# Forgetting attention on TensorE: two heads scored in the two halves of the array's rows, values formed once per pair

## The chip, the cores and the metric

The kernel runs on one core of one Trainium2 chip. The metric is device time in microseconds of one execution; lower is better. The shape is fixed: one sequence of 512 tokens, width 1024, one launch for the whole program.

## What is computed

Two transformer-like blocks in a row. Only the attention of the second block changes. It has 16 heads of 64 channels, 512 queries and keys, a causal mask, and a "forget" term: a running sum `c` per head and key that is added to the scores before the softmax.

```
def forgetting_attention(q, k, v, c):
    ...
    def one_block(args):
        q_i, c_i, i = args
        s = jnp.einsum('bhqd,bhkd->bhqk', q_i, k, preferred_element_type=jnp.float32) * scale
        s = s + c_i[..., None] - c[:, :, None, :]
        qpos = i * Q_BLOCK + jnp.arange(Q_BLOCK)
        s = jnp.where(kpos[None, :] <= qpos[:, None], s, -jnp.inf)
        p = jax.nn.softmax(s, axis=-1)
        return jnp.einsum('bhqk,bhkd->bhqd', p.astype(v.dtype), v)
```

(`c_i` is the same for a whole row of scores, so the softmax doesn't see it; the kernel adds only the key's part.) Keys and queries come from projections with a norm per head; the result is multiplied by a sigmoid gate and projected by `b_w_out`.

## The kernel before, in words

**Matmuls of the projections.** All weights are fp32. A weight tile is split into a rounded part `wh` (ScalarE, L181) and the rest `wl` (VectorE, L182), an activation tile likewise into `xh` and `xl`, and each product is three matmuls of 128x128 by 128x512 (L202, L203, L204 in `mm3`). One output tile `mm` is 8 such triples. There are three pairs of `wh`/`wl` buffers, so a split waits until TensorE has finished with the pair three tiles earlier.

**Attention before.** Heads lie in pairs, 64 channels each in one tile of 128 partitions (`KN[i]`, `pairs[i]`). For each head, `stack` builds stacked operands of 128 rows: `qa` and `ka` hold the rounded part in one half of the rows and, in the other half, the rest of the query and a copy of the rounded key; `qb` and `kb` hold the rounded query against the rest of the key, and in rows 64 to 111 the forget sums against a selecting column. So `scores` of a head and a block `tb` of 128 queries is two matmuls of up to 128 rows (L1279, L1280) over the `w = 128 (tb + 1)` keys seen so far, and a bf16 matmul of a mask with the identity over the diagonal block (L1281). VectorE takes the row maximum `nmx` (L1283), `powers` is an exponential on ScalarE, `shares` multiplies by the reciprocal of the sum (GpSimd for `tb` 0 and 1, VectorE for 2 and 3, L114), `turn` transposes each 128x128 piece on TensorE (`pt`, L1305) and copies it out on ScalarE (`et`, L1307), and `values` multiplies with the values (`ao`, L1317): fp32 matmuls of 128 rows by 64 columns of the array, head A into output partitions 0 to 63, head B into 64 to 127. Each fp32 matmul of that kind stands in the trace as two records.

**What sets the order.** `weave` interleaves two generators: `main` (query and gate projections, in the order `ORDER`, after `QL` queries that run ahead) and `side` (the attention, 64 steps of one head and one block, `LAG` steps between scores and transposes, `VLAG` steps between transposes and values). `ATT` holds their weights. A scheduler then places each engine's instructions in a fixed order; at run time every engine works through its own list and waits where an operand or a buffer is not ready. PSUM has 8 banks for all of it. The last stretch, `residual("bo", ...)`, uses the gated pairs after they are split (`OS`).

One place in the first block matters for the prediction. L742 in `Core.mid` issues fp32 matmuls of 128 rows by 32 columns of the array in turn for two column groups (output partitions 0 to 31 and 32 to 63), each over 64 moving columns.

Of the kernel before, what the change touches and what calls it, by code (L numbers as in the profile page):

```python
# [8 lines left out]
F32 = mybir.dt.float32  # L9
F32R = mybir.dt.float32r  # L10
BF16 = mybir.dt.bfloat16
# [9 lines left out]
NT = 4  # L21
# [7 lines left out]
N_T = 51  # L29
N_S = 10  # L30
N_T2 = 6
XA = 14

LOOK = 2

# [22 lines left out]
def tile_two_blocks(ctx: ExitStack, tc: tile.TileContext, a: dict, out: bass.AP):  # L58
# [23 lines left out]
    def PS(name="p", shape=(128, 512)):  # L82
        return pp.tile(list(shape), F32, tag="p", name=nm(name))
# [997 lines left out]
    def bcast_a():  # L1081
# [11 lines left out]
    cmask = T("cmask", (128, 128))  # L1093
    pool.memset(cmask, 0.0)
    pool.affine_select(out=cmask, in_=cmask, compare_op=ALU.is_ge, fill=NEG, base=0,
                       pattern=[[-1, 128]], channel_multiplier=1)
    cm16 = cp.tile([128, 128], BF16, name="cm16")
    pool.tensor_copy(cm16, cmask)
    id16 = cp.tile([128, 128], BF16, name="id16")
    pool.tensor_copy(id16, ident)  # L1100


    cr = xp[-1].tile([48, 512], F32R, tag="x", name="cr")
    pool.memset(cr.bitcast(F32), 0.0)
    sel = T("sel", (48, 16))
    pool.memset(sel, 0.0)
    for q in (0, 32):
        dve.tensor_copy(sel[q:q + 16, :], ident[q:q + 16, q:q + 16])
    selr = cp.tile([48, 16], F32R, name="selr")
    dve.tensor_copy(selr, sel)  # L1110

    def forget(p):
        z = T("fz", (16, 512))
        tt(dve, z, p[:16, :], nrm["rb"][:16, :])
        ts(dve, z, z, bft[:, 0:1], ALU.add)
        e = T("fe", (16, 512))
        stt(e, z, -1.0, z, ALU.mult, ALU.min)
        f(e, e, AF.Exp)
        f(e, e, AF.Ln, bias=1.0)
        stt(e, z, 0.0, e, ALU.min, ALU.subtract)  # L1120
        on = T("on", (16, 512))
# [4 lines left out]
        stt(cr[32:48, :], cs, -1.0, cr[0:16, :].bitcast(F32), ALU.mult, ALU.subtract)  # L1126

    kqs = cp.tile([128, 2], F32, name="kqs")
    ts(dve, kqs[:, 0:1], V("kn"), -0.5, ALU.mult)
# [105 lines left out]
            i, hn = summed.pop(0)  # L1235
            pairs[i] = hn.out()

    kbs = [xp[-1].tile([128, 512], F32R, tag="kb", bufs=2, name=nm("kb")) for _ in range(2)]
    for t in kbs:
        dve.tensor_copy(t[64:112, :], cr.bitcast(F32))  # L1240
    stacks, parts = {}, []

    def stack(h):

        i, hA = divmod(h, 2)
        qn, kn = pairs[i], KN[i]
        if hA:
            pairs.pop(i)
        u = slice(64 * hA, 64 * hA + 64)
        w = slice(64 - 64 * hA, 128 - 64 * hA)  # L1250
        qa, ka, qb = (xp[-1].tile([128, 512], F32R, tag="x", name=nm(s)) for s in ("qa", "ka", "qb"))
        kb = kbs[h % len(kbs)]
        stacks[h] = (qa, ka, qb, kb)
# [20 lines left out]
    def scores(h, tb):  # L1274
        qa, ka, qb, kb = stacks[h]
        w = (tb + 1) * 128
        p = PS("sc")
        tsl = slice(tb * 128, (tb + 1) * 128)
# [3 lines left out]
        nmx = SM("nmx", 1)  # L1282
        dve.tensor_reduce(out=nmx, in_=p[:, :w], axis=AX.X, op=ALU.max, negate=True)  # L1283
        return p, nmx

    def powers(h, tb, p, nmx):
        w = (tb + 1) * 128
        e = XT("pe")
        ssum = SM("sum", 1)
        f(e[:, :w], p[:, :w], AF.Exp, bias=nmx, accum=ssum)  # L1290
        sums.append((h, tb, e, ssum))

    def shares():
        h, tb, e, ssum = sums.pop(0)
        w = (tb + 1) * 128
        rs = SM("rs", 1)
        dve.reciprocal(rs, ssum)  # L1297
        ts(pool if tb in SHARE_POOL else dve, e[:, :w], e[:, :w], rs, ALU.mult)
        es[h, tb] = e

    def turn(h, tb):
        e = es.pop((h, tb))
# [4 lines left out]
        act.copy(et[:, :(tb + 1) * 128], pt[:, :(tb + 1) * 128])  # L1307
        ets[h, tb] = et

    def values(h, tb):  # L1310
        i, hA = divmod(h, 2)
        if i not in outs:
            outs[i] = PS("ao")
        o = outs[i]
        et = ets.pop((h, tb))
        for j in range(tb + 1):
            pe.matmul(o[64 * hA:64 * hA + 64, tb * 128:(tb + 1) * 128],  # L1317
                      lhsT=v[j][h // 8][:, (h % 8) * 64:(h % 8) * 64 + 64],
                      rhs=et[:, j * 128:(j + 1) * 128], start=(j == 0), stop=(j == tb))

    def side():
        def wait(i):
            while i not in pairs:
                yield None

        yield from wait(0)
        for part in stack(0):
            part()
        for _ in range(HEADSTART):
            yield None  # L1330
        for n in range(64 + LAG + VLAG):
            m = n - LAG
            k = m - VLAG
            if n % 4 == 0 and n < 60:
                yield from wait((n // 4 + 1) // 2)
                parts.extend(stack(n // 4 + 1))
            if n < 64:
                p, nmx = scores(*divmod(n, NT))
                yield 55 + 107 * (n % NT + 1)
            if sums:  # L1340
                shares()
            if 0 <= m < 64:
                turn(*divmod(m, NT))
                yield 107 * (m % NT + 1)
            if n < 64:
                powers(*divmod(n, NT), p, nmx)
            if parts:
                parts.pop(0)()
            elif turns["g"] == 8 and len(OS) < len(OG):
                OS.append(split(OG[len(OS)]))  # L1350
            if k >= 0:
                values(*divmod(k, NT))
                if k % 4 == 3:
                    stacks.pop(k // 4)
                if k % 8 == 7:
                    i = k // 8
                    while i not in gates:
                        yield None
                    t = T("og")
                    tt(dve, t, outs.pop(i), gates.pop(i))  # L1360
                    OG.append(t)
                    if i == 7:
                        for q in range(len(OS), 8):
                            OS.append(split(OG[q]))
                yield 214 * (k % NT + 1)

    def main():
        for k in ORDER:
# [37 lines left out]
```

## Time and profile before

| what | value |
|---|---|
| median of 3 runs | 2132.24 us (2131.89 to 2133.09) |
| profiled execution, its time | 2132.8 us |
| profiled execution, its span | 2131.1 us |
| TensorE busy | 2087.4 us, 98% of the span, 11200 matmuls |
| VectorE / ScalarE / GpSimd busy | 57% / 41% / 23% |
| attention with the woven projections | about 1541 to 1727 us from the span's start |

The span runs from the first to the last instruction. A busy TensorE is not one at its peak: matmuls are pipelined, records overlap, and what a matmul costs is read from the distance between the starts of neighbours, not from its duration.

### The profile page before, as it was taken

To read this page: it belongs to the slowest core of one execution; us is meant where nothing else is said; L and a number is where in the kernel's file an instruction comes from. 1 tells how busy PE (TensorE), PEld (TensorE's weight loads), DVE (VectorE), ACT (ScalarE), POOL (GpSimd) and SP (SyncE) were. 2 spreads that over 40 slices of the span, in tenths; PEclk is the share of its full clock that TensorE was granted. 3 is DMA by queue.
4 is the path that set the end of the run, shared out by engine and by line. 5 is a ranking of instruction groups with operands and counts; after the bars stand their busy time and mean duration, and the time that the engine had idled before them with its cause. 6 is when DMAs were issued, how large, how long until landed. Compare 5 with 4: busy or idle time off the path is not lost.

```text
span 2131.1 us, 27353 instructions
## 1 busy us (share of the span) xinstructions
PE 2087.4 (98%) x11200; PEld 1710.1 (80%) x11200; DVE 1221.2 (57%) x1636; ACT 880.2 (41%) x1362; POOL 493.9 (23%) x440
## 2 busy tenths in 40 slices
PE   8998888999999999999999999999999999999999
PEld 7877677888888888888888888878877778888887
DVE  4698787555344443664654453568587765545453
ACT  5456555543323323422333232345466644323232
POOL 3555654012222222400210010120034311001000
PEclk9999989999999999999999999999999999999999
DMA  6221111332233332323232233233311112323221
GB/s 219 90 70 41 61 60 60 99 115 86 97 99 99 99 97 82 99 79 119 80 114 91 93 99 99 80 101 99 98 41 41 40 60 79 107 91 108 90 89 50
DMA packets 179190, 187.54 MB, mean 88 GB/s; under 512 B 4379, under 2 KB 169976, under 8 KB 179064
## 3 DMA queue, kind: packets, MB, share of 16 engines
q1 hardware_dynamic: 179048, 185.79, 27.1%
q8 instruction: 88, 1.44, 0.3%
q14 instruction: 38, 0.31, 0.0%
q10 hardware_dynamic: 16, 0.00, 0.0%
HBM read 183.68 MB, written 2.10 MB: 87 GB/s over the span
## 4 chain that ended last, share of the span: by engine, by line
PE 91%; DVE 5%; ACT 2%; POOL 1%; issue 1%; DMA 0%; SPq 0%; POOLq 0%; ACTq 0%; DVEq 0%
PE mm L202 26%; PE mm L203 26%; PE mm L204 26%; PE ao L1317 2%; PE mn L244 1%; PE mn L243 1%; PE mn L242 1%; DVE dec L107 1%; DVE wl L182 1%; POOL dec L107 1%; PE pt L1305 1%; DVE sc L107 1%; PE sc L1279 1%; PE ml L229 1%; PE ml L228 1%
## 5 line engine op out<-in xcount | busy, mean ns | idle before, releaser
L202 PE MATMUL mm<-xh,wh 128*128 128x512 f32 x2552 | 1000.7, 393 | 0.0
L203 PE MATMUL mm<-xl,wh 128*128 128x512 f32 x2552 | 996.1, 391 | 2.9 <-DVE xl L107 2.9
L204 PE MATMUL mm<-xh,wl 128*128 128x512 f32 x2552 | 995.9, 391 | 0.0
L181 ACT CAST wh<-raw 128x1024 fp32r<-128x1024 f32 (+2 forms) x355 | 363.7, 1025 | 782.2 <-PE mm L203 695.2
L182 DVE TENSOR_TENSOR wl<-raw,wh 128x1024 fp32r<-128x1024 f32 (+2 forms) x355 | 469.5, 1323 | 187.0 <-ACT wh L181 182.6
L203 PEld LDWEIGHTS mm<-xl,wh 128*128 128x128 f32 x2552 | 479.3, 188 | 103.1 <-DVE xl L107 3.2
L202 PEld LDWEIGHTS mm<-xh,wh 128*128 128x128 f32 x2552 | 479.1, 188 | 102.2 <-issue 1.7
L204 PEld LDWEIGHTS mm<-xh,wl 128*128 128x128 f32 x2552 | 479.3, 188 | 100.7 <-issue 0.5
L107 POOL TENSOR_TENSOR ua<-ua,rb 128x512 f32<-128x512 f32 x44 | 57.3, 1302 | 592.6 <-ACT ua L120 592.6
L107 DVE TENSOR_TENSOR x<-mm,x 128x512 f32<-128x512 f32 x64 | 44.1, 691 | 153.0 <-PE mm L204 153.0
L107 POOL TENSOR_TENSOR dec<-sc 128x256 f32<-128x256 f32 x96 | 85.6, 921 | 30.0 <-DVE sc L652 23.4
L107 POOL TENSOR_TENSOR acc<-acc,sq 128x512 f32<-128x512 f32 x42 | 66.4, 1583 | 105.1 <-ACT sq L120 84.0
L107 DVE TENSOR_TENSOR a<-mm,rb 128x512 f32<-128x512 f32 x44 | 30.4, 691 | 103.8 <-PE mm L204 103.8
L107 POOL TENSOR_TENSOR rl<-rl 128x512 f32<-128x512 f32 x32 | 49.2, 1537 | 129.1 <-ACT rl L120 129.1
L107 DVE TENSOR_TENSOR sg<-mm,ua 128x512 f32<-128x512 f32 x44 | 30.4, 690 | 83.9 <-POOL ua L107 81.4
L114 POOL TENSOR_SCALAR pe<-pe,rs 128x128 f32<-128x128 f32 (+1 forms) x32 | 31.0, 969 | 188.8 <-DVE rs L1297 183.4
L110 DVE SCALAR_TENSOR_TENSOR ua<-a,convs,ua 128x511 f32<-128x511 f32 x88 | 65.8, 748 | 4.8 <-ACT ua L120 3.3
L120 ACT ACTIVATE ua<-ua 128x512 f32<-128x512 f32 x44 | 27.8, 632 | 86.9 <-DVE ua L110 86.9
L242 PE MATMUL mn<-wh,xh 128*128 128x512 f32 x160 | 63.2, 402 | 0.0
L243 PE MATMUL mn<-wl,xh 128*128 128x512 f32 x160 | 62.9, 393 | 0.0
L244 PE MATMUL mn<-wh,xl 128*128 128x512 f32 x160 | 60.8, 390 | 0.0
L107 DVE TENSOR_TENSOR rs<-mm,rb 128x512 f32<-128x512 f32 x32 | 22.0, 688 | 60.1 <-PE mm L204 60.1
(259 smaller groups left out, 1984.0 us busy)
## 6 DMA issues: line engine op xcount, KB each, us to landing
raw<-in_ffn_w_up_dram SPq DMA_DIRECT2D x44, 1024.0 KB
raw<-in_w_ff_dram SPq DMA_DIRECT2D x32, 1024.0 KB
raw<-in_w_in_dram SPq DMA_DIRECT2D x26, 1024.0 KB
raw<-in_ffn_w_down_dram SPq DMA_DIRECT2D x18, 1024.0 KB
raw<-in_a_w_in_dram SPq DMA_DIRECT2D x12, 1024.0 KB
raw<-in_w_kvf_dram SPq DMA_DIRECT2D x8, 1024.0 KB
raw<-in_b_w_qg_dram SPq DMA_DIRECT2D x8, 1024.0 KB
raw<-in_w_up_b_dram SPq DMA_DIRECT2D x4, 1024.0 KB
```

The costliest lines, as they stand in the source:

```text
L107: e.tensor_tensor(out=o, in0=i0, in1=i1, op=op)
L110: dve.scalar_tensor_tensor(out=o, in0=i0, scalar=s, in1=i1, op0=op0, op1=op1)
L114: e.tensor_scalar(out=o, in0=i, scalar1=s1, scalar2=None, op0=op0)
L181: act.copy(hi, src)
L182: ins = dve.tensor_tensor(out=lo, in0=src, in1=hi.bitcast(F32), op=ALU.subtract)
L202: pe.matmul(ps, lhsT=lh, rhs=rh, start=start, stop=False)
L203: pe.matmul(ps, lhsT=lh, rhs=rl, start=False, stop=False)
L204: pe.matmul(ps, lhsT=ll, rhs=rh, start=False, stop=stop_)
L242: pe.matmul(pss[j], lhsT=xh[:, t0], rhs=wh[:, kk, :], start=(k + kk == 0), stop=False)
L243: pe.matmul(pss[j], lhsT=xh[:, t0], rhs=wl[:, kk, :], start=False, stop=False)
L244: pe.matmul(pss[j], lhsT=xl[:, t0], rhs=wh[:, kk, :], start=False, stop=(k + kk == nk - 1))
L1317: pe.matmul(o[64 * hA:64 * hA + 64, tb * 128:(tb + 1) * 128], lhsT=v[j][h // 8][:, (h % 8) * 64:(h % 8) * 64 + 64], rhs=et[:, j * 128:(j + ...
```

## The change

`stack` is built once per pair: the key tile and the query tile of the pair (128 partitions, both heads) are each split once into `kh`, `kl`, `qh`, `ql`. `scores` handles both heads of a pair for one block: three products of 64 rows for each head (`qh kh`, `ql kh`, `qh kl`), head A in rows 0 to 63 of the array and head B in rows 64 to 127, each into its own PSUM bank; a matmul over 48 rows that adds the forget sums; and the mask as two bf16 matmuls of 64 rows by 64 columns for each head. `values` runs once per pair, after its four blocks, and takes the two heads in turn. The steps are 32 instead of 64, `LAG` and `VLAG` are counted in those, and four queries run ahead of the weave instead of three.

```diff
-XA = 14
+XA = 18
...
-LAG = 4
-VLAG = 3
-QL = 3
-ORDER = "gqgqgqgqgqggg"
+LAG = 2
+VLAG = 1
+QL = 4
+ORDER = "gqgqgqgqgggg"
...
-ATT = (70, 72)
+ATT = (70, 66)
...
-    def stack(h):
-
-        i, hA = divmod(h, 2)
-        qn, kn = pairs[i], KN[i]
...
-        def high():
-            act.copy(ka[u, :], kn[u, :])
-            act.copy(qa[u, :], qn[u, :])
-
-        def low_k():
-            tt(dve, kb[0:64, :], kn[u, :], ka[u, :].bitcast(F32), ALU.subtract)
-            pool.tensor_copy(qb[64:112, :], selr[:, h:h + 1].bitcast(F32).to_broadcast([48, 512]))
-
-        def low_q():
-            tt(dve, qa[w, :], qn[u, :], qa[u, :].bitcast(F32), ALU.subtract)
-
-        def twice():
-            dve.tensor_copy(ka[w, :], ka[u, :].bitcast(F32))
-            dve.tensor_copy(qb[0:64, :], qa[u, :].bitcast(F32))
-
-        return [high, low_k, low_q, twice]
+    def stack(i):
+
+        qn, kn = pairs.pop(i), KN[i]
+        qh, kh, ql, kl = (RX(s) for s in ("qh", "kh", "ql", "kl"))
+        stacks[i] = (qh, ql, kh, kl)
+
+        def part(src, hi, lo):
+            act.copy(hi, src)
+            tt(dve, lo, src, hi.bitcast(F32), ALU.subtract)
+
+        return [lambda: part(kn, kh, kl), lambda: part(qn, qh, ql)]
...
-        pe.matmul(p[:, :w], lhsT=qa[:, tsl], rhs=ka[:, :w], start=True, stop=False)
-        pe.matmul(p[:, :w], lhsT=qb[:112, tsl], rhs=kb[:112, :w], start=False, stop=False)
-        pe.matmul(p[:, tsl], lhsT=id16, rhs=cm16, start=False, stop=True)
+        for n, (q, k) in enumerate(((qh, kh), (ql, kh), (qh, kl))):
+            for u in range(2):
+                pe.matmul(ps[u][:, :w], lhsT=q[half[u], tsl], rhs=k[half[u], :w], start=(n == 0), stop=False)
+        for u in range(2):
+            r = slice(64 * u, 64 * u + 48)
+            pe.matmul(ps[u][:, :w], lhsT=selr[r, 2 * i + u:2 * i + u + 1].to_broadcast([48, 128]), rhs=cr[r, :w],
+                      start=False, stop=False)
+        for n in range(2):
+            for u in range(2):
+                c0 = tb * 128 + 64 * n
+                pe.matmul(ps[u][:, c0:c0 + 64], lhsT=picks[half[u], n, :], rhs=steps[half[u], :], start=False,
+                          stop=(n == 1))
...
-    def values(h, tb):
...
+    def values(i):
+
+        o = outs[i] = PS("ao")
+        for tb in range(NT):
+            ts_ = [ets.pop((2 * i + u, tb)) for u in range(2)]
+            for j in range(tb + 1):
+                for u in range(2):
+                    h = 2 * i + u
+                    pe.matmul(o[64 * u:64 * u + 64, tb * 128:(tb + 1) * 128],
+                              lhsT=v[j][h // 8][:, (h % 8) * 64:(h % 8) * 64 + 64],
+                              rhs=ts_[u][:, j * 128:(j + 1) * 128], start=(j == 0), stop=(j == tb))
```

Besides, constants are made differently (`steps` and `picks` in place of the mask and the bf16 identity, `selr` and `cr` over 112 rows), and one reciprocal takes both heads of a pair.

How the instructions stand now, at three places. First TensorE in the middle of the attention. Before, a head's scores, transposes (`pt`) and values (`ao`) alternate in small pieces with the projections:

```order
L1281 MATMUL sc_12451<-cm_11116,id_11118 128x128
L1317 MATMUL ao_12258<-et_12375,v_11744 64x128
L1151 MATMUL hn_12429<-hsl_12316,bones 128x512
L1317 MATMUL ao_12258<-et_12375,v_11746 64x128
L1317 MATMUL ao_12258<-et_12375,v_11748 64x128
L1317 MATMUL ao_12258<-et_12375,v_11750 64x128
L1305 MATMUL pt_12460<-ident,pe_12347 128x128 x3
```

Of the change, a pair's values stand in one piece, the two heads (two `et` tiles) in turn:

```order
L1319 MATMUL ao_12948<-et_12682,v_11756 64x128
L1319 MATMUL ao_12948<-et_12686,v_11756 64x128
L1319 MATMUL ao_12948<-et_12771,v_11756 64x128
L1319 MATMUL ao_12948<-et_12776,v_11756 64x128
L1319 MATMUL ao_12948<-et_12771,v_11758 64x128
L1319 MATMUL ao_12948<-et_12776,v_11758 64x128
```

Over the whole program the column-half matmuls `ao` make 61 separate visits before and 11 now (8 pairs, two of them cut into more pieces). The score matmuls on row halves, which did not exist before, make 34 visits, with 43 stretches of full-array work around them all.

Second, TensorE at a pair's scores. In most of the 32 blocks the heads alternate, here in the block of 512 keys of one pair (`sc_12984` head A, `sc_12985` head B):

```order
L1270 MATMUL sc_12984<-kh_12602,qh_12601 128x512
L1270 MATMUL sc_12985<-kh_12602,qh_12601 128x512
L1270 MATMUL sc_12984<-kh_12602,ql_12603 128x512
L1270 MATMUL sc_12985<-kh_12602,ql_12603 128x512
L1270 MATMUL sc_12984<-kl_12604,qh_12601 128x512
L1270 MATMUL sc_12985<-kl_12604,qh_12601 128x512
L1273 MATMUL sc_12984<-cr,selr 128x512
L1273 MATMUL sc_12985<-cr,selr 128x512
```

In 7 of the 32 (three of 128 keys, one of 256, three of 384) the scheduler has put all of head A ahead of all of head B, as here with 256 keys; in 2 more, of 384 keys, the first four stand as A A B B:

```order
L1270 MATMUL sc_12847<-kh_12602,qh_12601 128x256
L1270 MATMUL sc_12847<-kh_12602,ql_12603 128x256
L1270 MATMUL sc_12847<-kl_12604,qh_12601 128x256
L1273 MATMUL sc_12847<-cr,selr 128x256
...
L1270 MATMUL sc_12848<-kh_12602,qh_12601 128x256
L1270 MATMUL sc_12848<-kh_12602,ql_12603 128x256
L1270 MATMUL sc_12848<-kl_12604,qh_12601 128x256
L1273 MATMUL sc_12848<-cr,selr 128x256
```

Third, ScalarE where the weave begins, at the norm of the last query that runs ahead (`hs`, `hsh` are its square and the rounded square, for which TensorE's `hn` waits). Before, with the weight split `wh_12108` ahead of them:

```order
L181 CAST wh_12108<-raw_12106 128x1024 [waits DMAHW5_49,PE_49]
L120 ACTIVATE hr_12021<-hm_12019 128x512 [waits DVE_49]
L120 ACTIVATE hs_12032<-hn_12030 128x512 [waits DVE_49,Activation_49]
L120 ACTIVATE hr_12021<-hr_12021 128x512 [waits Activation_49]
L1145 CAST hsh_12034<-hs_12032 128x512 [waits Activation_49]
```

Of the change, one tile later in the program, the same five in the same order:

```order
L180 CAST wh_12171<-raw_12046 128x1024 [waits PE_49]
L119 ACTIVATE hr_12080<-hm_12078 128x512 [waits DVE_49]
L119 ACTIVATE hs_12091<-hn_12089 128x512 [waits DVE_49]
L119 ACTIVATE hr_12080<-hr_12080 128x512 [waits Activation_49]
L1152 CAST hsh_12093<-hs_12091 128x512 [waits Activation_49]
```

## Rows read from the trace of the kernel before

**Rows 1.** The page, part 1: busy us, share of the span, instructions.

```profile
PE 2087.4 (98%) x11200; PEld 1710.1 (80%) x11200; DVE 1221.2 (57%) x1636; ACT 880.2 (41%) x1362; POOL 493.9 (23%) x440
```

**Rows 2.** Windows: length, busy (count) of PE, PEld, DVE, ACT, POOL; TensorE clock; DMA.

```profile
1540.00:1560.00 20.00, 16.77 (x80) 12.67 (x78) 17.53 (x34) 12.15 (x26) 2.41 (x3) 0.91 0.17 53
...
1600.00:1620.00 20.00, 20.00 (x118) 14.99 (x117) 16.79 (x36) 13.62 (x36) 7.28 (x8) 1.00 0.00 1
```

**Rows 3.** Waits of TensorE from 1520 to 1740 us: total, times, longest.

```profile
PE hn L1150 <- ACT hsh L1145: 3.0, 1, 3.0
PE ao L1317 <- ACT et L1307: 0.7, 1, 0.7
PE pt L1305 <- POOL pe L114: 0.7, 1, 0.7
```

**Rows 4.** Timeline of TensorE, undisturbed projections: start, us, instruction, count.

```profile
1593.39 0.40 PE L203 MATMUL mm<-xl,wh 128*128 128x512 f32 x1
1593.62 0.39 PE L204 MATMUL mm<-xh,wl 128*128 128x512 f32 x1
```

**Rows 5.** Timeline of TensorE, values of two blocks and their neighbours.

```profile
1607.12 0.65 PE L1317 MATMUL ao<-et,v 128*64 128x128 f32 x4
...
1610.96 0.50 PE L1305 MATMUL pt<-ident,pe 128*128 128x128 f32 x3
1611.39 1.09 PE L1317 MATMUL ao<-et,v 128*64 128x128 f32 x8
1612.41 0.50 PE L204 MATMUL mm<-xh,wl 128*128 128x512 f32 x1
1612.75 0.40 PE L1279 MATMUL sc<-ka,qa 128*128 128x512 f32 x1
1612.98 0.39 PE L1280 MATMUL sc<-kb,qb 112*128 112x512 f32 x1
1613.22 0.23 PE L1281 MATMUL sc<-cm,id 128*128 128x128 bf16 x1
1613.26 0.48 PE L202 MATMUL mm<-xh,wh 128*128 128x512 f32 x1
1613.57 0.39 PE L203 MATMUL mm<-xl,wh 128*128 128x512 f32 x1
```

**Rows 6.** Instructions by form, 1520 to 1740 us, and L742 in the first block.

```profile
L1317 PE MATMUL ao<-et,v 128*64 128x128 f32 x320 | 48.3, 283 | 0.8 <-ACT et L1307 0.7
...
135.10 0.61 PE L742 MATMUL lv<-dec 128*32 128x64 f32 x15
...
L742 PE MATMUL lv<-dec x128: 219/219/243, 135.0 to 344.0; 128*32 128x64 f32 x128
```

**Rows 7.** Timeline of TensorE, second score matmul and mask of three blocks.

```profile
1607.86 0.28 PE L1280 MATMUL sc<-kb,qb 112*128 112x128 f32 x1
1607.98 0.23 PE L1281 MATMUL sc<-cm,id 128*128 128x128 bf16 x1
...
1609.06 0.28 PE L1280 MATMUL sc<-kb,qb 112*128 112x256 f32 x1
1609.18 0.23 PE L1281 MATMUL sc<-cm,id 128*128 128x128 bf16 x1
...
1610.71 0.34 PE L1280 MATMUL sc<-kb,qb 112*128 112x384 f32 x1
1610.90 0.23 PE L1281 MATMUL sc<-cm,id 128*128 128x128 bf16 x1
```

**Rows 8.** VectorE and ScalarE groups by form, 1520 to 1740 us.

```profile
L107 DVE TENSOR_TENSOR qa<-hn,qa 64x512 fp32r<-64x512 f32 x16 | 12.1, 759 | 1.0 <-ACT qa L1257 0.9
...
L1283 DVE TENSOR_REDUCE nmx<-sc 128x1 f32<-128x512 f32 x16 | 10.9, 680 | 5.5 <-PE sc L1281 5.4
...
L120 ACT ACTIVATE pe<-sc,nmx 128x512 f32<-128x512 f32 x16 | 11.0, 689 | 9.2 <-DVE nmx L1283 7.9 <-DVE rs L1297 1.1
...
L1307 ACT COPY et<-pt 128x512 f32<-128x512 f32 x16 | 9.3, 582 | 2.3 <-PE pt L1305 1.6 <-PE sc L1279 0.6
```

More of the change, by code (lines that the diff above doesn't have):

```diff
@@ L1092, in tile_two_blocks @@
     dve.tensor_copy(bones, bo)
[L1093 to L1103, printed above, removed]
+    steps = cp.tile([128, 64], BF16, name="steps")
+    picks = cp.tile([128, 2, 128], BF16, name="picks")
+    pool.memset(picks, 0.0)
+    for u in (0, 64):
+        st = T("st", (128, 64))
+        pool.memset(st, NEG)
+        pool.affine_select(out=st, in_=st, compare_op=ALU.is_ge, fill=0.0, base=u, pattern=[[1, 64]],
+                           channel_multiplier=-1)
+        dve.tensor_copy(steps[u:u + 64, :], st[u:u + 64, :])
+        for n in range(2):
+            dve.tensor_copy(picks[u:u + 64, n, 64 * n:64 * n + 63], ident[u:u + 64, u + 1:u + 64])
+        pool.memset(picks[u:u + 1, 1, 0:64], 1.0)
+    cr = xp[-1].tile([112, 512], F32R, tag="x", name="cr")
     pool.memset(cr.bitcast(F32), 0.0)
-    sel = T("sel", (48, 16))
+    sel = T("sel", (112, 16))
     pool.memset(sel, 0.0)
-    for q in (0, 32):
+    for q in (0, 32, 64, 96):
         dve.tensor_copy(sel[q:q + 16, :], ident[q:q + 16, q:q + 16])
-    selr = cp.tile([48, 16], F32R, name="selr")
+    selr = cp.tile([112, 16], F32R, name="selr")
     dve.tensor_copy(selr, sel)
@@ L1272, in tile_two_blocks @@
+    def stack(i):
[6 more added lines that the diff above has]
+        return [lambda: part(kn, kh, kl), lambda: part(qn, qh, ql)]
     es, ets, outs, sums = {}, {}, {}, []
-    def scores(h, tb):
-        qa, ka, qb, kb = stacks[h]
+    half = [slice(0, 64), slice(64, 128)]
@@ L1293, in shares, with powers @@
+        for u in range(2):
+            dve.tensor_reduce(out=nmx[:, u:u + 1], in_=ps[u][:, :w], axis=AX.X, op=ALU.max, negate=True)
+        return ps, nmx
+    def powers(i, tb, ps, nmx):
+        w = (tb + 1) * 128
+        ssum = SM("sum", 2)
+        for u in range(2):
+            e = es[2 * i + u, tb] = XT("pe")
+            f(e[:, :w], ps[u][:, :w], AF.Exp, bias=nmx[:, u:u + 1], accum=ssum[:, u:u + 1])
+        sums.append((i, tb, ssum))
     def shares():
-        h, tb, e, ssum = sums.pop(0)
+        i, tb, ssum = sums.pop(0)
@@ L1295, in shares @@
         w = (tb + 1) * 128
-        rs = SM("rs", 1)
+        rs = SM("rs", 2)
         dve.reciprocal(rs, ssum)
-        ts(pool if tb in SHARE_POOL else dve, e[:, :w], e[:, :w], rs, ALU.mult)
-        es[h, tb] = e
+        for u in range(2):
+            e = es[2 * i + u, tb]
+            ts(pool if tb in SHARE_POOL else dve, e[:, :w], e[:, :w], rs[:, u:u + 1], ALU.mult)
     def turn(h, tb):
@@ L1308, in turn @@
         ets[h, tb] = et
-    def values(h, tb):
[L1311 to L1319, printed above, removed]
+    def values(i):
[3 more added lines that the diff above has]
+            for j in range(tb + 1):
+                for u in range(2):
+                    h = 2 * i + u
+                    pe.matmul(o[64 * u:64 * u + 64, tb * 128:(tb + 1) * 128],
+                              lhsT=v[j][h // 8][:, (h % 8) * 64:(h % 8) * 64 + 64],
+                              rhs=ts_[u][:, j * 128:(j + 1) * 128], start=(j == 0), stop=(j == tb))
     def side():
@@ L1330, in side @@
             yield None
-        for n in range(64 + LAG + VLAG):
+        for n in range(32 + LAG + VLAG):
             m = n - LAG
             k = m - VLAG
[L1334 to L1339, printed above, removed]
+            i, tb = divmod(n, NT)
+            if n < 32:
+                ps, nmx = scores(i, tb)
+                yield 100 + 214 * (tb + 1)
@@ L1340, in side @@
             if sums:
                 shares()
[L1342 to L1346, printed above, removed]
+            if 0 <= m < 32:
+                for u in range(2):
+                    turn(m // NT * 2 + u, m % NT)
+                yield 214 * (m % NT + 1)
+            if n < 32:
+                powers(i, tb, ps, nmx)
+                if tb == 0 and i < 7:
+                    yield from wait(i + 1)
+                    parts.extend(stack(i + 1))
+                if tb == 3:
+                    stacks.pop(i)
@@ L1347, in side @@
             if parts:
                 parts.pop(0)()
-            elif turns["g"] == 8 and len(OS) < len(OG):
+            if turns["g"] == 8 and len(OS) < len(OG):
                 OS.append(split(OG[len(OS)]))
[L1351 to L1365, printed above, removed]
+            if k >= 0 and k % 4 == 3:
+                i = k // 4
+                values(i)
+                while i not in gates:
+                    yield None
+                t = T("og")
+                tt(dve, t, outs.pop(i), gates.pop(i))
+                OG.append(t)
+                if i == 7:
+                    for q in range(len(OS), 8):
+                        OS.append(split(OG[q]))
+                yield 2500
```

28 lines of the change are left out of this document (8 added, 20 removed).

## The prediction
> **What bounds the kernel now.** I read the page first, then windows of 20 us around the attention, TensorE's waits there, and its timeline matmul by matmul. TensorE is busy 98% of the span, all others below 60% [rows 1]. In the attention it is just as full: 20.00 of 20 us from 1600 to 1620, at full clock, with VectorE at 17 and ScalarE at 14 [rows 2]. Its waits from 1520 to 1740 us come to 4.4 us, of which 3.0 are one wait at the start of the weave [rows 3]; the clock falls to 0.91 in that window [rows 2]. So the kernel is bound by what TensorE issues, and the change is worth what it takes from or adds to that list. Busy time does not tell a matmul's price, since records overlap: a projection matmul lasts 0.40 us, but the next starts 0.23 us later [rows 4]. All prices below are distances between starts.
>
> **Part 1, the values.** There are 160 fp32 matmuls of 64 array columns, 320 records [rows 6]. One record costs (1.09 - 0.65) / 4 = 0.11 us [rows 5], all of them 35.2 us. Now the two heads, which write different column halves, stand in turn. Two column groups in turn are in the trace: at L742 15 records of 64 moving columns take 0.61 us, one alone 0.22 us, so a record costs (0.61 - 0.22) / 14 = 0.028 us [rows 6]. A value record has 128 columns and 0.11 us, so 0.055 for 64: taken in turn, two records pass in the time of one. The 320 then cost 17.6 us, a gain of **17.6 us**. Ends: 0 if halves of 64 columns don't overlap as groups of 32 do, 17.6 if they do. I take 17.6, since L742 is the same data type, the same 128 rows and two streams.
>
> **Part 2, visits.** Going from full-array matmuls to column halves and back is not free. In the burst at 1611 us the three transposes before take 0.43 us for 0.33, the eight records 1.02 us (to the start of the next) for 0.88, and the projection behind 0.34 us for 0.23 [rows 5]: 0.10 + 0.14 + 0.11 = 0.35 us for a visit, 0.175 for a change of shape. Before, 61 visits make 122 changes. Now there are 11 such visits and 34 to row halves between 43 full stretches, 87 changes. No row shows a change to row halves; its ends are 0 (34 x 0.35 = 11.9 us more gain) and some more than 0.175. The nearest row is the column visit, and I take its price: 35 changes fewer, a gain of **6.1 us**. The Trainium skill ("TensorEngine Tiling (Array Packing)", Key Properties) says that a change of tiling mode drains TensorE, which speaks against a kernel that now uses three shapes; by that rule row visits are not free, as I took it, and the trace agrees for columns with its 0.35 us.
>
> **Part 3, the scores.** Before, a head's block costs two matmuls over w keys; the second's start to the mask's is 0.12, 0.12, 0.19 and 0.24 us for 128, 256, 384 and 512 keys [rows 5, 7], 0.67 us in all. Per pair that is 2 heads x 2 x 0.67 = 2.7 us, 21.4 us for 8 pairs. Now each head has four such matmuls of 64 or 48 rows. If the two heads overlap in their row halves, the pair takes four slots, the same 21.4 us; if they don't, eight, **21.4 us more**. The trace of before has no row halves, so these are the ends; the nearest row is again the pair of column groups, which overlap fully, and I take overlap. The skill's page has row tiles work side by side too ("TensorE: Matmul & The Clock Gate", Part 3: four tiles measured at 3.07 times the speed of one); no run here shows it yet. But overlap needs the heads in turn. In 7 of 32 blocks (three of 128 keys, one of 256, three of 384) all of A stands before all of B: there four slots are added, 4 x (3 x 0.12 + 0.12 + 3 x 0.19) = 4.2 us, and two blocks in the order A A B B add 0.19 each. A loss of **4.6 us**.
>
> The mask before: 0.04 us to the next start, and the projection behind it takes 0.31 for 0.23 [rows 5], so 0.12 us, 64 times, 7.7 us. Now there are 128 of half the length, most in overlapping pairs. Ends: 64 x 0.04 = 2.6 us and 128 x 0.12 = 15.4; I take 7.7, no difference, as the weight load behind, not the columns, seems to set the 0.12.
>
> **Part 4, the other engines.** The pair's tiles are split once: VectorE loses the 32 splits of half tiles (0.76 us each [rows 8]) and 32 copies for 16 splits of whole tiles, ScalarE 32 roundings for 16, GpSimd 16 copies. I cost this at nothing: TensorE's work covers it. What is left on them must come in time: for 512 keys two maxima, two exponentials and two copies (0.68, 0.69 and 0.58 us each [rows 8]), one head behind the other, which had more time between them before. The distance from scores to transposes is two steps of a pair, as long as four of a head. A block's two score tiles and two transposed tiles now hold 4 of 8 banks at once, and the tail has one pair's values at the end instead of single blocks. I put **3 us** on new waits, about as often again as the 1.4 us beside the start [rows 3] and a little for the tail, ends 0 and 8. The 3.0 us at the start stay: ScalarE's list has the weight split, which waits for TensorE, ahead of the square as before, one tile later. With it stays the clock's dip. The fourth early query only moves along TensorE's list; the weight loads follow, with DMA at 0.00 to 0.17 of its time here [rows 2]. The new constants are a few short operations in front of full work.
>
> **Sum.** -17.6 - 6.1 + 4.6 + 3 = -16.1 us. The profiled execution took 2132.8 us, 1.7 over its span and 0.6 over the median of the runs; 2132.8 - 16.1 = 2116.7, by the median **2116 us**.
>
> **The rivals.**
> - *Row halves run one behind the other.* For it: nothing in the trace shows rows side by side. Against it: column groups do overlap. The 25 blocks in turn lose as well: 21.4 - 4.6 = 16.8 us on top, 2116 + 17 = **2133**, no change.
> - *Each half's weight load shows.* Each matmul needs its own load; if a half's load can't run under that half's own matmul, each of 4 x 4 x 8 = 128 slots shows about 0.12 us, the least spacing of two score matmuls whose columns are few [rows 7]: 15 us, **2131**. Against it: a projection loads new weights for every matmul in all rows and still follows in 0.23 us, while the same array streams [rows 4]. The skill ("TensorE: Matmul & The Clock Gate", Part 3, The mechanism) says that a load overlaps with running matmuls only when the row group differs; rows 4 speak against that in the strict sense, so it gets a small chance.
> - *Column halves of 64 don't overlap.* Only part 1 falls: 2116 + 18 = **2134**. L742 speaks against it.
> - *A wait takes TensorE's place.* The second score matmul of a block stands behind a bank that ScalarE's copy or exponential must free, and everything on TensorE stands behind it. With 3 us of waits in the sum already, the change turns slower (over 2136.5) once each of 32 steps waits 0.7 us, one exponential of 512 keys [rows 8]; at 0.8 us it is 2116 - 3 + 26 = **2139**. For it: the banks, and ScalarE at 14 of 20 us [rows 2]. Against it: before, with the same 8 banks, all waits for copies and shares come to 1.4 us [rows 3], and VectorE has less to do.
> - *The change does not act at all* is no case of its own: the order shows other instructions, and the two ways in which they would cost the same are the first and third rival.
>
> **Chances and range.** The forecast 0.78, row halves in a row 0.06, loads that show 0.05, column halves 0.03, waits 0.08. Within 0.2%, about what a measurement can tell from no change (4.3 us, 2128 to 2136.5), lie the first three rivals, 0.14; slower 0.08; faster 0.78. The forecast's own range: free row visits or cheaper masks give up to 8 to 12 us more, waits and masks up to 8 less, 2106 to 2126. To leave out no more than 2 in 10 the upper end reaches the rivals near 2131, the lower is cut to 2107, since several ends would have to come together: 2107 to 2131.
>
> **What would show it.** Right: two heads' score matmuls start within a few hundredths of each other and the next two one slot (0.24 us for 512 keys) later; value records 0.055 us apart on the mean; about 0.35 us more around each visit to row halves; new waits of TensorE under 5 us. Wrong: even spacing of 0.24 us between the heads' scores (first rival), 0.12 us more on every slot (second), 0.11 us between value records (third), or a row of TensorE's waits with 32 entries for ScalarE or VectorE (fourth). A gain over 25 us would mean that row visits cost nothing.

## The result and the profile after

The changed kernel takes 2117.47 us (median of 4 runs, 2116.10 to 2119.79), the kernel before 2132.06 (4 runs): ratio 0.9933, 95% interval 0.9916 to 0.995, faster by 14.6 us. The prediction said 2116 and 2107 to 2131. The profiled execution took 2119.79 us, its span is 2118.0.

The page of the changed kernel, part 1, answers to [rows 1]: TensorE is still the bound, with 192 more instructions and 14.8 us less busy time.

```profile
PE 2072.6 (98%) x11392; PEld 1703.6 (80%) x11392; DVE 1196.6 (56%) x1567; ACT 869.8 (41%) x1347; POOL 476.4 (22%) x423
```

The changed kernel's TensorE timeline: a block of 512 keys, the first projections after the scores of the next block, then the values of a pair (start, us, instruction, count):

```profile
1608.16 0.50 PE L1270 MATMUL sc<-kh,qh 64*128 64x512 f32 x2
1608.50 0.40 PE L1270 MATMUL sc<-kh,ql 64*128 64x512 f32 x2
1608.74 0.40 PE L1270 MATMUL sc<-kl,qh 64*128 64x512 f32 x2
...
1609.21 0.23 PE L1278 MATMUL sc<-steps,picks 64*128 64x64 bf16 x4
1609.38 0.66 PE L1306 MATMUL pt<-ident,pe 128*128 128x128 f32 x4
...
1610.91 0.50 PE L201 MATMUL mm<-xh,wh 128*128 128x512 f32 x1
1611.25 0.40 PE L202 MATMUL mm<-xl,wh 128*128 128x512 f32 x1
...
1620.05 0.39 PE L202 MATMUL mm<-xl,wh 128*128 128x512 f32 x1
1620.37 0.44 PE L1270 MATMUL sc<-kh,qh 64*128 64x384 f32 x2
...
1621.71 2.40 PE L1319 MATMUL ao<-et,v 128*64 128x128 f32 x40
1624.04 0.50 PE L203 MATMUL mm<-xh,wl 128*128 128x512 f32 x1
```

The two heads' matmuls stand together as x2. The second two start 0.34 us behind the first, which carry a part of the visit, and from there on the step is 0.23 to 0.24 us, that of one matmul alone: the row halves overlap fully. 40 value records take 2.33 us, 0.058 each, for 0.11 before [rows 5]. A visit to row halves shows at three places: 0.32 us ahead of its first matmul (1620.05 to 1620.37) and 0.34 behind the first full-array matmul after it (1610.91 to 1611.25), where a projection takes 0.23, and 0.34 for 0.24 inside. That makes 0.09 + 0.10 + 0.11 = 0.30 us, a little less than a column visit.

Windows of the changed kernel, columns as in [rows 2]:

```profile
1540.00:1560.00 20.00, 14.04 (x53) 10.51 (x51) 11.60 (x16) 6.87 (x11) 0.00 (x0) 0.83 0.19 56
1560.00:1580.00 20.00, 20.00 (x124) 14.64 (x123) 16.34 (x37) 13.85 (x40) 3.46 (x4) 0.74 0.15 50
```

The waits of TensorE from 1500 to 1740 us come to 8.2 us; before they were 4.4 [rows 3]:

```profile
PE hn L1157 <- ACT hsh L1152: 6.0, 2, 3.0
PE mm L201 <- ACT xh L477: 2.2, 1, 2.2
```

The start is worse than before: there are two waits of 3.0 us for one, and the mean clock of the two windows is 0.83 and 0.74, where it was 0.91 [rows 2] and 1.00. The timeline of ScalarE there shows what stands ahead of both waits:

```profile
1544.21 1.04 ACT L180 CAST wh<-raw 128x1024 fp32r<-128x1024 f32 x1 [2.25 <-PE mm L202]
1546.73 0.60 ACT L1152 CAST hsh<-hs 128x512 fp32r<-128x512 f32 x1
1556.12 1.04 ACT L180 CAST wh<-raw 128x1024 fp32r<-128x1024 f32 x1 [8.79 <-PE mm L202]
1558.64 0.60 ACT L1152 CAST hsh<-hs 128x512 fp32r<-128x512 f32 x1
```

Each time `hsh` stands behind a weight split that waits for TensorE, and TensorE's `hn` then waits for `hsh`. Behind the first wait 12 projection matmuls start 0.43 us apart instead of 0.23, the lower of the clock's two levels (1.2 for 2.4 GHz):

```profile
1548.41 0.63 PE L202 MATMUL mm<-xl,wh 128*128 128x512 f32 x1
1548.83 0.63 PE L203 MATMUL mm<-xh,wl 128*128 128x512 f32 x1
```

Behind the second wait the lower level holds from about 1560 to about 1570 us.

**Where the time went.** I summed the distances from each TensorE start to the next by the group of the first matmul, from 1500 us up to and with the last `ao`; what a distance has above 0.55 us is put down as waiting. (`mm` holds the projections; what a change of shape or the mask costs a neighbour is counted at the neighbour.)

| us (matmuls) | before | change | late | b_values | b_q4 |
|---|---|---|---|---|---|
| values `ao` (320) | 44.3 | 19.9 | 19.5 | 19.4 | 19.7 |
| scores and mask `sc` | 29.4 (192) | 32.6 (384) | 32.4 (384) | 35.8 (192) | 33.3 (192) |
| projections `mm` | 102.6 (412) | 102.4 (393) | 95.5 (393) | 94.4 (384) | 91.0 (384) |
| waiting | 3.7 | 7.9 | 2.2 | 18.4 | 9.3 |

The last three columns are experiments below. From before to the change the values give 24.4 us, scores take 3.2 and waits 4.2. The last `ao` starts 17.5 us earlier (1725.3, 1707.8), but 19 projections that stood ahead of it now stand behind, 4.4 us at 0.23: 13.1 us net. The spans of the two profiled executions differ by just that (2131.1, 2118.0); the medians differ by 14.6. A projection takes 0.249 us on the mean before, 0.261 in the change, 0.243 in 'late': 393 x 0.012 = 4.7 us more than before. I put that down to the lower clock, since with the same 393 projections 'late', which keeps full clock there, has 6.9 us less.

### The profile page after: what moved, and what is told of

Its sections match the earlier page's. It is cut to its first block, busy times and chain, and to the rows that moved or that the text cites. A ratio compares the mean times of both kernels' runs of the same rounds, so it can differ in the third digit from the quotient of the medians.

```text
span 2118.0 us, 27605 instructions
## 1 busy us (share of the span) xinstructions
PE 2072.6 (98%) x11392; PEld 1703.6 (80%) x11392; DVE 1196.6 (56%) x1567; ACT 869.8 (41%) x1347; POOL 476.4 (22%) x423
## 4 chain that ended last, share of the span: by engine, by line
PE 88%; DVE 7%; POOL 2%; ACT 2%; issue 1%; DMA 0%; SPq 0%; POOLq 0%; DVEq 0%; ACTq 0%
PE mm L201 26%; PE mm L202 26%; PE mm L203 25%; POOL dec L106 2%; PE mn L242 1%; PE mn L243 1%; PE mn L241 1%; DVE dec L106 1%; DVE sc L106 1%; PE sc L1270 1%; DVE wl L181 1%; PE ao L1319 1%; ACT e L119 1%; PE pt L1306 1%; PE ml L228 1%
## 5 line engine op out<-in xcount | busy, mean ns | idle before, releaser
L109 DVE SCALAR_TENSOR_TENSOR xl<-x,vecs,xh 128x512 fp32r<-128x512 f32 x40 | 55.8, 1399 | 5.0 <-ACT xh L119 4.8
```

## The experiments

My theory after the result: values, visits and the rows' overlap are as predicted, and the start of the weave costs some 13 us, 6.0 by its two waits and 7 by the clock. The rivals are that the gain has another source (fewer splits, an earlier query), or that the halves overlap whatever their order. Intervals are those of the ratio to the kernel before.

**Values, heads one behind the other** (v_apart), so that 63 of 159 neighbours change half instead of all:

```diff
-            for j in range(tb + 1):
-                for u in range(2):
+            for u in range(2):
+                for j in range(tb + 1):
```

> The changed kernel, but in values each block takes head A's matmuls and then head B's. Of the 159 pairs of neighbours in the values, 63 now change from one column half to the other, before this edit all 159. My theory: each change of half lets one record of 0.11 us pass beside another, so 96 x 0.11 = 10.5 us come back: 2117.5 + 10.5 = 2128 us, and value records 0.09 us apart on the mean instead of 0.058. Rival: the values gained by their fewer visits alone, and the halves overlap however they stand or not at all: 2117 to 2118 us, spacing unchanged.

2125.15 us, 0.9963 (0.9948 to 0.9977): 7.7 us slower than the change, 10.5 expected. The groups by form of the change and of this run (busy, mean ns):

```profile
L1319 PE MATMUL ao<-et,v 128*64 128x128 f32 x320 | 20.3, 276 | 0.0
```

```profile
L1319 PE MATMUL ao<-et,v 128*64 128x128 f32 x320 | 25.7, 283 | 0.0
```

By starts the values take 25.3 us for 19.9. The order of the heads is what the overlap hangs on. The loss is smaller than expected because a change of half that comes seldom hides more than one record: without the 1.5 us that visits take inside the values (11 x 0.14), 35.2 us have become 23.8, which is 0.18 us, or one and a half records of 0.11, for each of the 63 changes (an estimate).

**Scores, all of head A, then all of B, in all 32 blocks** (s_apart):

```diff
-        for n, (q, k) in enumerate(((qh, kh), (ql, kh), (qh, kl))):
-            for u in range(2):
+        for u in range(2):
+            for n, (q, k) in enumerate(((qh, kh), (ql, kh), (qh, kl))):
...
```

The forget sums and the masks of a head stand in the same loop now, behind its three products.

> The changed kernel, but in scores all matmuls of head A stand before all of head B, in all 32 blocks instead of 7. My theory: row halves overlap when the heads stand in turn and only partly otherwise. In the trace of the change the blocks with the heads apart cost 0.28, 0.36 and 0.46 us more (128, 256, 384 keys) than those in turn; with an estimated 0.6 for 512 keys, 25 more blocks cost 5 x 0.28 + 7 x 0.36 + 5 x 0.46 + 8 x 0.6 = 11 us: 2128 us. Rival one, a list strictly in order, where only the last of A meets the first of B, or no overlap: 16 us or more, 2134. Rival two, the order within a block does not matter: 2117 to 2118 us.

2131.01 us, 0.9995 (0.9986 to 1.0005): 13.5 us slower than the change, so nearly the whole gain is gone. That lies between the theory's 11 us and the 16 of its first rival. The TensorE timeline of this run at 512 keys:

```profile
1629.37 0.49 PE L1270 MATMUL sc<-kh,qh 64*128 64x512 f32 x1
1629.70 0.39 PE L1270 MATMUL sc<-kh,ql 64*128 64x512 f32 x1
1629.93 0.39 PE L1270 MATMUL sc<-kl,qh 64*128 64x512 f32 x1
1629.93 0.49 PE L1270 MATMUL sc<-kh,qh 64*128 64x512 f32 x1
1630.16 0.40 PE L1272 MATMUL sc<-cr,selr 48*128 48x512 f32 x1
...
1631.14 0.50 PE L201 MATMUL mm<-xh,wh 128*128 128x512 f32 x1
```

A block of 512 keys takes 1.77 us (1629.37 to 1631.14) for 1.22 in turn (1608.16 to 1609.38). Of the four slots that could be lost, little more than two are (0.55 us at 0.24): B's first starts with A's third, ahead of A's `cr` and A's masks, which the program lists before it. So it is in 30 of the 32 blocks. How far A may run ahead at no cost, the change shows. In two of the seven blocks that the text ahead of the prediction counts as apart (one of 128 keys, one of 384), the list has A's three products, then B's three, then the forget sums in turn; there B's first starts with A's first, and the blocks take 0.67 and 0.99 us, as those in turn do (0.67 and 0.97). Only the other five, with all of A ahead of all of B, lose time.

**The norm sums of a query issued two projections later** (late), so that ScalarE has squared it long before:

```diff
-        while held:
-            i, hn = held.pop(0)
+        while held and held[0][0] < tiles[0]:
+            _, i, hn = held.pop(0)
...
-START = 7
+START = 5
```

> The changed kernel, but the norm sums of a query are issued two projection tiles later (after five of eight triples of the second next tile) instead of one. My theory: the two waits of 3.0 us at the start of the weave come from ScalarE's list, where a weight split that waits for TensorE stands ahead of the norm's square; they also let the clock fall, so that about 15 us run at half clock, which costs 12 projections x (0.43 - 0.23) = 2.4 us after the first wait and about 4.6 us after the second. Without them 6.0 + 7.0 = 13 us less, some given back by later queries: 2105 to 2109 us, clock 1.00 from 1540 to 1580. Rival: the wait moves to the scores, since queries come later: 2114 us or more.

2105.92 us, 0.9877 (0.9862 to 0.9892): 11.5 us faster than the change. Its waits from 1500 to 1740 us and its windows at the start:

```profile
PE pt L1309 <- DVE pe L113: 2.0, 2, 1.2
PE mm L201 <- ACT xh L477: 0.6, 1, 0.6
PE pt L1309 <- POOL pe L113: 0.6, 1, 0.6
PE pt L1309 <- ACT hr L119: 0.5, 1, 0.5
```

```profile
1540.00:1560.00 20.00, 20.00 (x112) 15.61 (x111) 19.18 (x34) 13.60 (x30) 2.65 (x3) 1.00 0.33 105
1560.00:1580.00 20.00, 18.91 (x155) 14.64 (x153) 14.20 (x31) 11.82 (x34) 9.15 (x8) 1.00 0.01 2
```

There is no wait for `hsh`, and the clock is full. The start is worth about what the theory says: 11.5 us, of which waits give 5.7 and projections 6.9 in the table, and other groups take some back.

**The same in the kernel before** (before_late; the edit is that of 'late'):

> The kernel before with the late norm sums of the experiment 'late', nothing of the change. Its list has 97 changes of array shape where before has 122, because the scheduler places the values otherwise. Theory (before lost only 3.0 us of wait and 0.09 x 20 = 1.8 us of clock at the start, the change lost 6.0 of wait and more of the clock): 3.0 + 1.8 + 25 x 0.175 = 9 us less than before, about 2123 (2120 to 2126), so that with the start undisturbed in both the change is worth 2123 - 2105.9 = 17 us, near the 19 of the prediction's terms without waits (17.6 + 6.1 - 4.6). Rival (the start costs both kernels the same, late is worth its 11.5 us here too, and changes of shape on top): 2116 or less, the change is worth 10. Rival (late helps only by what it moves in the changed kernel): 2132, the change is worth 26.

2132.00 us, 0.9999 (0.999 to 1.0008). My number missed, and the time is the last rival's: the `hsh` wait goes, but the waits of TensorE show another in its place, and the clock of 1540 to 1560 us is 0.87.

```profile
PE sc L1282 <- DVE qa L107: 5.4, 2, 4.7
```

With 'late' in both the change is worth 26.1 us. In the kernel before, the operands of the first pair's second head were due next (`qa`, 4.7 us), so nothing was gained.

**Only the values of the change** (b_values: the kernel before with a pair's values in one piece, heads in turn, 18 changes of shape in the trace):

```diff
...
-                values(*divmod(k, NT))
+                if k % 8 == 7:
+                    values(k // 8)
...
```

> The kernel before, with one part of the change alone: values once per pair, the two heads in turn; scores, steps and lags as before. My theory, by the terms of the prediction: values 17.6 us less, and visits, with 17 changes of shape instead of 122, 105 x 0.175 = 18.4 us less; some waits of the tail come back, 2 us: 2132 - 34 = 2098 us, better than the change, which spends 68 changes of shape on its row halves and nothing else on TensorE is gained by them. Rival: visits cost nothing once they hold more matmuls, or cost only what the values themselves lose: 2113 to 2116 us.

2125.81 us, 0.997 (0.9958 to 0.9983): 28 us above my number. TensorE's list did shrink (`ao` 19.4 us for 44.3), but waits took the place. Its waits from 1500 to 1740 us:

```profile
PE sc L1279 <- DVE qa L107: 11.5, 5, 3.3
PE pt L1305 <- POOL pe L114: 4.4, 6, 1.9
PE hn L1150 <- ACT hsh L1145: 3.0, 1, 3.0
```

So the same values give 25 us of TensorE's list and only 6 us of time here. Two causes were open: VectorE's splits per head, which the change halves, or something upstream. The next four tell them apart.

**More VectorE work in the changed kernel** (dve_more: 'late' with each low part subtracted three times):

```diff
             act.copy(hi, src)
-            tt(dve, lo, src, hi.bitcast(F32), ALU.subtract)
+            for _ in range(3):
+                tt(dve, lo, src, hi.bitcast(F32), ALU.subtract)
```

> The kernel of 'late' with each of the 16 low parts of queries and keys subtracted three times over: 32 x 0.69 = 22 us more of VectorE work in the way of the operands of the scores, about what splitting once per pair took away (VectorE's busy time fell from 1221 to 1197 us). Theory (b_values failed because the operands of the scores came too late once TensorE's list was shorter, so that the fewer splits are what lets the change keep its gain): waits of TensorE for kl, ql, nmx or pe appear, 6 to 15 us, 2112 to 2121. The prediction's step (this work is covered by TensorE's and costs nothing): 2106, within 2 us.

2118.77 us, 0.9938 (0.9921 to 0.9955): 12.9 us slower than 'late'. VectorE's 22 us, work and delay together, are not covered by TensorE's. But the waits come at the shares more than at the operands:

```profile
PE pt L1310 <- POOL pe L113: 5.2, 6, 2.5
PE pt L1310 <- DVE pe L113: 2.5, 2, 1.3
PE sc L1274 <- DVE ql L106: 1.3, 2, 1.1
```

**The copies of b_values' operands on GpSimd** (b_pool: `pool.tensor_copy` for `dve.tensor_copy` in `twice`), 15 us off VectorE:

> The kernel of 'b_values' with the copies of the operands into the other half of rows (32 of 0.48 us) on GpSimd, where VectorE had them. Theory (VectorE's list, not the latency of one operand, is late): 15 us leave VectorE, the waits for qa fall by a half or more of their 11.5 us, 2114 to 2121. Rival (each operand's own chain is late: GpSimd's copies take longer than VectorE's, its copy of 48 rows takes 0.81 us): waits for qb or ka on GpSimd in the place of those for qa, 2125 or more.

2129.33 us, 0.9989 (0.998 to 0.9999): slower than b_values. TensorE waits only 0.2 us for GpSimd's copies, and still for `qa`, so neither the theory nor the rival is right.

```profile
PE sc L1279 <- DVE qa L107: 8.5, 5, 2.0
PE hn L1150 <- ACT hsh L1145: 5.8, 3, 3.0
```

**b_values with the late sums** (b_late):

> The kernel of 'b_values' (the kernel before, with the values per pair and the heads in turn, as the only part of the change) with the late norm sums of 'late'. Theory (what holds b_values up are the operands qa, ka, qb and kb, which VectorE makes for each head apart, and not the wait at the start): the 3.0 us for hsh go, the waits for qa stay or grow, 2120 to 2127. Rival (the start and its clock hold it up, as in the changed kernel): 11 us go, 2112 to 2115, and the split once per pair is not needed for the gain.

2129.43 us, 0.999 (0.998 to 0.9999), a little above the theory's range: the start is not what holds it up either. The timeline of b_values shows what `qa` stands behind, at the fifth pair:

```profile
1612.38 0.69 DVE L110 SCALAR_TENSOR_TENSOR hn<-hm,hn 128x512 f32<-128x512 f32 x1 [1.43 <-POOL hm L107]
1613.11 0.62 ACT L1257 CAST qa<-hn 64x512 fp32r<-64x512 f32 x1 [1.05 <-DVE hn L110]
1614.16 0.69 DVE L107 TENSOR_TENSOR qa<-hn,qa 64x512 fp32r<-64x512 f32 x1
...
1615.00 0.30 PE L1279 MATMUL sc<-ka,qa 128*128 128x128 f32 x1 [1.61 <-DVE qa L107]
```

The pair's query itself is normed only 1.9 us ahead of its first score. From the end of that `hn<-hm,hn` to the pair's first score matmul, pairs 4 to 8:

| us | pair 4 | 5 | 6 | 7 | 8 |
|---|---|---|---|---|---|
| before | 21.3 | 10.3 | 9.2 | 9.3 | 3.7 |
| b_values | 2.9 | 1.9 | 1.5 | 1.5 | 1.5 |
| b_pool | 11.0 | 2.5 | 1.5 | 1.5 | 1.6 |
| change | 38.5 | 28.5 | 22.6 | 16.7 | 10.7 |
| b_q4 | 25.2 | 13.4 | 4.4 | 3.9 | 1.9 |

**b_late with a fourth early query** (b_q4), as the change has it:

```diff
-QL = 3
-ORDER = "gqgqgqgqgqggg"
+QL = 4
+ORDER = "gqgqgqgqgggg"
```

> The kernel of 'b_late' with a fourth query projected and normed ahead of the weave, as the change has it, and nothing else of the change beside the values. In 'b_values', 'b_late' and 'b_pool' the norm of a pair's query ends 1.5 to 3.3 us before that pair's first score matmul from the fourth or fifth pair on, in the changed kernel 10.7 to 38.5 us before it. Theory (the query comes too late once TensorE's list is shorter, and the fourth early query is what cures it): the waits for qa go, most pairs have over 6 us between the query's norm and the first score matmul, and the time falls to what TensorE's list allows, about 2132 - 4.8 (start) - 24.9 (values: 44.3 us of starts in before, 19.4 in b_values) + 3 to 8 of waits = 2105 to 2111. Rival (VectorE's work on the operands of each head is what is late, as the run with more VectorE work suggests): waits for qa of 5 us and more, 2122 to 2130.

2110.21 us, 0.9893 (0.9876 to 0.9909): 19.2 us faster than b_late. The waits for `qa` fall but don't all go, and VectorE is busy 18.4 to 19.0 of 20 us from 1620 to 1680:

```profile
PE sc L1282 <- DVE qa L107: 4.5, 4, 2.4
PE pt L1308 <- POOL pe L114: 3.0, 5, 1.2
PE pt L1308 <- DVE pe L114: 2.9, 2, 1.6
```

So in the kernel before, with the values of the change, the fourth early query is what lets the shorter list count. All the rest of the change, splits and row halves among it, is the difference to 'late': 4.3 us more. These runs do not part the splits from the row halves, and no run takes the fourth early query out of the changed kernel itself.

**The price of a visit** (v_block: 'late' with values per block; 136 changes of shape in the trace for 84):

```diff
...
+            if k >= 0:
+                values(k // 4, k % 4)
...
             if k >= 0 and k % 4 == 3:
                 i = k // 4
-                values(i)
...
```

> The kernel of 'late' with the values issued per block of 128 queries, the two heads still in turn: 38 visits to column halves for 10, 134 changes of shape for 82, 8 blocks of scores with A ahead of B for 6. Theory (a change of shape costs 0.175 us): 52 x 0.175 = 9.1 us and about 0.8 for the two blocks more, 2105.9 + 9.9 = 2116 (2113 to 2119). Rival (the visits cost what they show only because a matmul's own length hides there; the gain of the change came from the turns alone): 2106 to 2108. Rival (values that come earlier take waits away): below 2106.

2116.82 us, 0.9929 (0.9914 to 0.9944): 10.9 us slower than 'late', 9.9 expected. The 0.175 us per change of shape holds about: (10.9 - 0.8) / 52 = 0.19. Its timeline shows the values of one block, 0.33 us behind the start of the projection ahead, and 0.59 us for eight records where 8 x 0.058 = 0.46:

```profile
1585.97 0.40 PE L203 MATMUL mm<-xh,wl 128*128 128x512 f32 x1
1586.30 0.66 PE L1323 MATMUL ao<-et,v 128*64 128x128 f32 x8
1586.89 0.50 PE L201 MATMUL mm<-xh,wh 128*128 128x512 f32 x1
```

**The mask left out** (no_mask, on 'late'):

```diff
-                      start=False, stop=False)
-        for n in range(2):
...
+                      start=False, stop=True)
```

> The kernel of 'late' without the mask's 128 matmuls, so that later keys count in every row of the scores. In the trace of the change the four masks of a block take 0.17 us from start to start (1609.21 to 1609.38): 32 x 0.17 = 5.4 us less, and about 2 more for 10 blocks with A ahead of B instead of 6 and 88 changes of shape instead of 82, 2105.9 - 3.5 = 2102.4 (2100 to 2104.5). By the prediction's 7.7 us for the masks: 2100. Rival (they lie beside other work and cost nothing): 2106 to 2109.

2105.54 us, 0.9877 (0.9861 to 0.9894): no difference to 'late', where I expected 3.5 us less. In its timeline a block of 512 keys takes 1.15 us (1611.10 to 1612.25):

```profile
1611.10 0.51 PE L1273 MATMUL sc<-kh,qh 64*128 64x512 f32 x2
...
1611.90 0.41 PE L1276 MATMUL sc<-cr,selr 48*128 48x512 f32 x2
1612.25 0.50 PE L201 MATMUL mm<-xh,wh 128*128 128x512 f32 x1
```

With the masks it was 1.22, so they cost 0.07 us a block and not the 0.17 from their first start to the next group's: 32 x 0.07 = 2.2 us. At the tail TensorE waits 2.3 us for `xh` now, for 0.6 in 'late', which takes most of them back.

**Scores kept in turn** (late_turn: the order of the score matmuls pinned, so that in the trace no block has all of A ahead of B, for six in 'late'):

```diff
-                pe.matmul(ps[u][:, :w], lhsT=q[half[u], tsl], ...)
+                pin(pe.matmul(ps[u][:, :w], lhsT=q[half[u], tsl], ...))
```

> The kernel of 'late' with the score matmuls kept in the order in which they are written, so that 30 of 32 blocks alternate between the heads, for 23. By the blocks of the trace of 'late' (1.54 for 0.67 us at 128 keys, 1.11 for 0.74 at 256, 1.43 for 0.97 at 384) the seven cost about 3 us: 2105.9 - 3 = 2103 (2101.5 to 2104.5). Rival (the scheduler put A ahead of B because B's bank came free later, and keeping the order makes TensorE wait for it): 2106 or more, with waits of sc for ACT or DVE.

2105.58 us (2104.49 to 2106.19), 0.9876 (0.9862 to 0.9891): not to be told from 'late'. By starts `sc` fell from 32.4 to 31.0 us, half of the 3 expected. A part of my estimate was a misreading: a block of 128 keys that I had counted as 1.54 us for its order has the heads in turn, and holds a wait of 0.80 us for `pe`. Where the rest of the 1.4 us went is not shown. Both versions beat the kernel before and the change.

## Why the prediction was right

The total was right within 1.5 us, and the mechanisms of the three large terms are shown. But the steps on the start of the weave, on the fourth early query and on the other engines failed, and errors of the opposite sign, in the scores and the visits, covered a part of what that cost. So close a hit is in part luck.

- **Values, -17.6.** This was right. By the prediction's own prices the group `ao` had to lose 17.6 us and, for 50 column visits fewer, the 0.14 us of each that stand inside the values [rows 5], 24.6 us in all; it lost 24.4. That the order of the heads makes the overlap is shown by v_apart.
- **Visits, -6.1.** This was right in kind: v_block gives 0.19 us a change of shape for 0.175. The price of a row visit, which no row of before showed, reads 0.30 us in the change for the 0.35 assumed. The count was two short (89 changes in the trace for 87, 0.35 us). With 50 column visits fewer at 0.35 and 34 row visits at 0.30 the term is -7.3. The Trainium skill's rule ("TensorEngine Tiling (Array Packing)", Key Properties), that a change of tiling mode drains TensorE, agrees with these runs.
- **Scores, overlap and +4.6.** The overlap was right: row halves run side by side, and with all of A ahead of all of B the gain is gone (s_apart). The loss was put too high. Such a block costs 0.28, 0.36 or 0.46 us more (128, 256, 384 keys) and not four slots (0.48, 0.48, 0.76), except one of 128 keys where other work stands between the heads; and blocks in which only two or three of A's stand ahead cost nothing to speak of. That makes about 2.0 us for five blocks.
- **Mask, 0.** The 7.7 us that I put on both sides were not confirmed: in no_mask the blocks without masks are 2.2 us shorter in all than those of 'late'. What the masks cost before is not tested by any run, so what the change made of it stays open.
- **New waits, +3.** The size was right and the reason wrong. Waits grew by 3.8 us, but by a second wait for `hsh` (3.0) and one for `xh` at the tail (2.2); the waits for copies and shares, which I had doubled, are gone.
- **"The 3.0 us at the start stay ... one tile later", and the clock's dip with it.** This failed. The wait did not move: it stands at 1547 us as before, for the third query, and the fourth early query has its own at 1559 us. The clock fell to 0.74 where it had been 1.00, which takes about 4.7 us by the projections. 'late' shows 11.5 us to be had there.
- **"The fourth early query only moves along TensorE's list".** This failed as well. The second wait is that query's, and an early query is what keeps operands ahead of a shorter list (b_late to b_q4: 19.2 us). Without it a wait takes TensorE's place, my fourth rival, though at the query's norm and not at the banks; that is shown on the kernel before with the new values, not on the change. (The fourth rival's own sum was off: 32 waits of 0.7 us make 2135.4, not over 2136.5.)
- **Other engines, nothing.** This does not hold by the test of dve_more: 22 us of VectorE's work, about what the single splits took away, cost 12.9 us when put back.

With these sizes the sum is -17.6 - 7.3 + 2.0 + 3.8 + 4.7 = -14.4 us, an estimate with the masks at nothing, beside 13.1 us between the profiled spans and 14.6 between the medians.

## What to carry to other kernels

When the bound engine's list gets shorter, everything that feeds it comes due earlier; ask of each input by how many microseconds it is early now, and subtract the gain as it adds up along the stage. A step that moves one producer ahead must be followed through each in-order queue, once per producer: a wait that one early query had, the next had too. In these runs work on halves of the array paid where the halves stood in turn, or had at most four matmuls of one ahead of the other, and in long visits.

## What the runs showed of the hardware that was not expected

TensorE starts a matmul on an idle row half ahead of one on the other half that the program lists before it: in s_apart B's first started at 1629.93 us, A's `cr` at 1630.16, and so in 30 of 32 blocks. Six of A's were listed ahead of B's first there, and it started with A's third. Where three were ahead of it (two blocks of the change), or four (three blocks of no_mask that nothing interrupts), it started with A's first: in all these blocks it started with the matmul that stands three or four places ahead of it. The Trainium skill ("TensorE: Matmul & The Clock Gate", Part 3, The mechanism) says that matmuls start strictly in program order; between the row halves of these runs they do not, and the measurement decides.

Each wait of 3.0 us cost more than its own length in the change: 12 projections behind the first, at 0.20 us more each, lost 2.4 us, and in the window behind the second the clock of 0.74 took (1 - 0.74) x 20 = 5.2 us. In the kernel before, the same 3.0 us wait left a window of 0.91, 1.8 us. In 'late', whose longest wait is 1.2 us, the clock of these windows stayed at 1.00.
